# Tokens of both norms turned into columns by VectorE and DRAM scratch instead of TensorE

## The chip, the cores and the metric

The kernel runs on one core of a Trainium2 chip. The core has five engines that run side by side, each with a queue of its own that it works off in order: TensorE (PE in the profile: matmuls, and PEld for its weight loads), VectorE (DVE), ScalarE (ACT), GpSimd (POOL) and SyncE (SP, which here only issues transfers). Transfers between DRAM and the on-chip memory SBUF go through 16 DMA engines. TensorE writes its results to the on-chip memory PSUM, and VectorE and ScalarE read them there.

The metric is the time of one execution in device microseconds. Before the change three runs gave a median of 994.76 us (994.67 to 995.08).

## The reference

One decoder layer over 1024 tokens of width 1024, in float32:

```python
z = h @ w_in                                   # pool group | q | k | v
mix = concat([pool_mixer(z), sliding_window_attention(z)]) @ w_out
h = layer_norm(ALPHA * h + mix, ln1_g, ln1_b)            # norm 1
ff = square(relu(h @ w_ff1)) @ w_ff2
h = layer_norm(ALPHA * h + ff, ln2_g, ln2_b)             # norm 2
gate = sigmoid(h @ w_ple_gate + b_ple_gate)
out = h + gate * (p @ w_ple)
```

What matters here are the two norms. A norm runs along the 1024 channels of a token, so it wants tokens on the 128 partitions and channels along the row. The matmul that follows (with `w_ff1` after norm 1, with `w_ple_gate` after norm 2) sums over channels, so it wants channels on the partitions and tokens along the row: columns. Between norm and matmul each tile of 128 tokens has to be transposed.

## The kernel before

The tokens come in 8 tiles of 128 (`NT = 8`), the channels in 8 blocks of 128 (`NK = 8`). Products are accurate to more than one pass: each operand is split into a high part (`high`, a rounding copy on ScalarE, line 98) and the low rest (`low`, a subtraction on VectorE, line 103), and `mm3` (lines 113 to 115) makes three matmuls of them. The feed-forward part further saves products by a 2x2 scheme with seven products instead of eight (token halves by channel halves), which needs sums and differences of column blocks.

The work is written in Python with a tile framework. A planner orders the instructions of each engine's queue before the run, by the place in the program and by a simulated clock, and gives each tile a free buffer of its pool. So the written order is a priority; the order in the queues is fixed when the kernel runs. Where `tc.issue_after` stands, an instruction is queued behind a named one.

The buffers that matter: tag "n" (`nat`, 8 of 4 KB per partition), tag "ws" (`part` and `incoming`, 6), tag "c" (`big`, 6), tag "t" (`temp`, 6), and banks of PSUM ("mm", "pt", "av", "s" in the first half, "f" in the second).

**Around norm 1.** `out_left` and `out_right` multiply by `w_out` into the halves of the token tiles `hn[n]`, four tiles (one token half, t = 0 or 1) at a time. `norm1(n)` then runs `layer_norm(hn[n])` on VectorE with one step on ScalarE and one on GpSimd, and turns the tile into columns: `transposed` (line 427) makes four 128x128 transposes on TensorE into a PSUM bank, once for channel blocks 0 to 3 (`a`, bank "pt") and once for 4 to 7 (`b`, bank "av"). After that the tile is scaled by ALPHA and written to DRAM as the residual (`h_dram`). From `a` and `b` it makes splits: for t = 0 the operands "11" and "21", and a copy of `a` for three tiles in `pre`; for t = 1 the operand "22" and the differences "T1", "T2", "T3" (and later, in `last_sum`, "T4"). In the written order, tiles 0 to 3 come after `out_left(1)`; tiles 4 to 7 alternate with `early(p)`, which multiplies the first weights of `w_ff1` with "11" and then "21" and so needs tiles 0 to 3. The products that need the "T" operands follow after the last `early`; the first of them is `s2`, with "T2".

**Around norm 2.** The second feed-forward matmul runs as 56 units (seven products `i`, eight quarters `q`, `k` counting the quarters of a product), the last product being `i == 2`. Its results are added into `acc[n]` by `gather`. `norm2(n)` is written for tiles 0 to 3 during the last two products, and for tiles 4 to 7 after them. The gate's weights are loaded and split in `gate_load` during the last product. `gate_in(n)` makes the columns of tile n: eight transposes on TensorE into two PSUM banks "f", then split into the pair `h2`. In the last loop, per tile: `gate_in(n + 1)`, then `ple` (12 matmuls with `w_ple`) and `gate` (48 matmuls) and `result`, which ends in a store by SP.

SP issues nearly all loads, so it is one queue in which a load that waits for a free buffer holds those behind it.

Of the kernel before, what the change touches and what calls it, by code (L numbers as in the profile page):

```python
# [7 lines left out]
F32 = mybir.dt.float32  # L8
# [4 lines left out]
P = 128  # L13
# [54 lines left out]
def layer(ctx, tc, xT, x, pT, w_in, w_pool, pscale, sinks, w_out, ln1, w1, w2, ln2, w_ple, w_gate, bgate, bias, rcount, out):  # L68
# [7 lines left out]
    def nm(s):  # L76
        uid[0] += 1
        return f"{s}_{uid[0]}"
# [7 lines left out]
    def nat(shape, dt=F32):  # L86
        return sb.tile(shape, dt, tag="n", bufs=8, name=nm("n"))
# [8 lines left out]
    def high(dst, src, scale=None):  # L96
        if scale is None:
            nc.scalar.copy(out=dst, in_=src)  # L98
        else:
            nc.scalar.mul(out=dst, in_=src, mul=scale)  # L100

    def low(eng, dst, src, hi):
        return eng.tensor_tensor(out=dst, in0=src, in1=hi.bitcast(F32), op=ALU.subtract)  # L103
# [13 lines left out]
    def add(o, a, b, op=ALU.add):  # L117
        nc.vector.tensor_tensor(out=o, in0=a, in1=b, op=op)  # L118
# [13 lines left out]


    h_dram = [tc.dram_tile([P, D], F32, name=f"hd{n}") for n in range(NT)]
    f_dram = [tc.dram_tile([P, 2, 2, 2, HALF], F32, name=f"fd{q}") for q in range(NQUAD - NKEEP)]


# [30 lines left out]
    def tr_ps():  # L168
        return ps.tile([P, 4, P], F32, tag="pt", bufs=2, name=nm("pt"))
# [248 lines left out]
        nc.vector.scalar_tensor_tensor(out=y, in0=y, scalar=r, in1=gb[0], op0=ALU.mult, op1=ALU.mult)  # L418
        add(y, y, gb[1])

    def tr_av():
        return ps.tile([P, 4, P], F32, tag="av", bufs=1, name=nm("av"))

    def transposed(y, j, pt):
        for k in range(4):
            kt = 4 * j + k
            nc.tensor.transpose(pt[:, k, :], y[:, kt * P : (kt + 1) * P], ident)  # L427
        return pt
# [86 lines left out]

    X = {}

    def block(name, i, c):
        return X[name][:, i, :, c * P : (c + 1) * P].bitcast(F32)

    def split_to(name, c, src, eng):
        cs = slice(c * P, (c + 1) * P)
        dh = X[name][:, 0, :, cs]
        high(dh, src)
        return low(eng, X[name][:, 1, :, cs], src, dh)

    def norm1(n):
        t, c = n // 4, n % 4
        layer_norm(hn[n], gb1)
        a = transposed(hn[n], 0, tr_ps())  # L530
        b = transposed(hn[n], 1, tr_av())
        nc.scalar.mul(out=hn[n], in_=hn[n], mul=ALPHA)
        nc.scalar.dma_start(out=h_dram[n], in_=hn[n])
        if t == 0:
            if c < 3:
                nc.scalar.copy(out=pre[:, 4 + c].rearrange("p (k t) -> p k t", k=4), in_=a)
            split_to("11", c, a, nc.vector)
            split_to("21", c, b, nc.vector)
        else:
            r12, t1, t2 = temp((P, 4, P)), temp((P, 4, P)), nat([P, 4, P])  # L540
            nc.scalar.copy(out=r12, in_=a)
            if c < 3:
                add(t1, a, pre[:, 4 + c].rearrange("p (k t) -> p k t", k=4), ALU.subtract)
# [85 lines left out]
    def bank(shape=(P, HALF)):  # L629
        return pf.tile(list(shape), F32, tag="f", bufs=8, name=nm("f"))  # L630
# [178 lines left out]
    def gate_load(j):  # L809
# [5 lines left out]
        for k in range(2):  # L815
            load_split(w[:, 0, k], w[:, 1, k], src[k * P : (k + 1) * P, :], None, nc.vector, incoming((P, D)))

    def gate_in(n):
        h2 = [part((P, NK, P)) for _ in range(2)]
        for j in range(2):  # L820
            pt = transposed(acc[n], j, bank((P, 4, P)))
            dh = h2[0][:, 4 * j : 4 * j + 4, :]
            high(dh, pt)
            low(nc.vector, h2[1][:, 4 * j : 4 * j + 4, :], pt, dh)
        return h2

    def norm2(n):
# [9 lines left out]
    for u, (i, q) in enumerate(units):  # L837
        k = QORDER.index(q)
        if u < NQUAD - NKEEP:
            hidden[u] = big([P, 2, 2, 2, HALF], F32)  # L840
            nc.sync.dma_start(out=hidden[u], in_=f_dram[u])
        if u == 4:
            quarter = wide("pre", [P, 4, D], F32)
            for n in range(4):
                acc.append(quarter[:, n])
                nc.sync.dma_start(out=acc[n], in_=h_dram[n])
        if i == 5 and k == 2:
            residual_back(2)
        if 4 <= u + 3 < len(units):
            fetch(u + 3)  # L850
        if u + 1 < len(units):
            prepare(u + 1)
        if k == 0:
            banks_of[i] = banks_of[MERGE[i]] if i in MERGE else [bank() for _ in range(4)]
        if i == 2 and k == 7:
            h2s = [gate_in(0)]
        multiply(u, banks_of[i])
        if i != 2 or k >= 5:
            for _ in range(2 if i == 2 else 1):
                if pending:  # L860
                    with tc.issue_after(lows[-1].ins):
                        pending.pop(0)()
        if k == 7:
            pending += [lambda c=c, i=i: gather(i, c, banks_of[i][c]) for c in range(4)]
        if i == 6:
            if k == 0:
                gb2 = [incoming((P, D)) for _ in range(2)]
                for j in range(2):
                    nc.sync.dma_start(out=gb2[j], in_=ln2[j].partition_broadcast(P))
            if k in (3, 6):  # L870
                norm2(k // 3 - 1)
        if i == 2:
            if k in (1, 4):
                norm2(2 + k // 3)
            if k == 2:
                residual_back(2)
            if k >= 2:
                gate_load(k - 2)
    for piece in pending:
        piece()  # L880

# [4 lines left out]
    for n in range(NT):  # L886
        if n + 1 < NT:
            h2s.append(gate_in(n + 1))
        h2 = h2s[n]
        cols = [slice(0, HALF), slice(HALF, D)] if n < NT - 1 else [slice(0, HALF), slice(HALF, HALF + HALF // 2), slice(HALF + HALF // 2, D)]  # L890

        def ple(cs):
            o = bank()[:, 0 : cs.stop - cs.start]
            for k in range(2):
                pk = pTs[:, :, k, n * P : (n + 1) * P]
                mm3(o, pk[:, 0], pk[:, 1], wl[:, 0, k, cs], wl[:, 1, k, cs], k == 0, k == 1)
            return o

        def gate(cs):
            o = bank()[:, 0 : cs.stop - cs.start]  # L900
            for k in range(NK):
                w = gates[k // 2]
                mm3(o, h2[0][:, k, :], h2[1][:, k, :], w[:, 0, k % 2, cs], w[:, 1, k % 2, cs], k == 0, k == NK - 1)
            return o

        def result(cs, gt, pl):
            sg = temp()[:, 0 : cs.stop - cs.start]
            nc.vector.tensor_tensor(out=sg, in0=b3[:, cs], in1=gt, op=ALU.add)
            nc.scalar.activation(out=sg, in_=sg, func=AF.Sigmoid)
            nc.vector.tensor_tensor(out=sg, in0=sg, in1=pl, op=ALU.mult)  # L910
            nc.vector.tensor_tensor(out=sg, in0=sg, in1=acc[n][:, cs], op=ALU.add)
            nc.sync.dma_start(out=out[n * P : (n + 1) * P, cs], in_=sg)

        if n == 0:
            gts = [gate(cs) for cs in cols]
            for cs, gt in zip(cols, gts):
                result(cs, gt, ple(cs))
        else:
            for cs in cols:
                if cs.stop == D and n == NT - 1:  # L920
                    gt = gate(cs)
                    result(cs, gt, ple(cs))
                else:
                    pl = ple(cs)
                    result(cs, gate(cs), pl)
# [46 lines left out]
```

## Time and profile before

| what | value |
|---|---|
| median of three runs | 994.76 us (994.67 to 995.08) |
| span of the profiled execution, first to last instruction | 993.0 us |
| PE idle time that waits on other engines | four waits, the longest 1.4 us |
| PE, 860 to 910 us | busy 50.0 of 50 us |
| DVE, 860 to 910 us | busy 47.0 of 50 us |
| DVE, 300 to 320 us | busy 19.6 of 20 us |

The page gives the span of one profiled execution, the busy time of each engine, and the chain of work that ended last, followed back from the last instruction. Below it stand groups of instructions: line, engine, operation, what is written and read (names without numbers), count, then busy time in us, mean duration of one in ns, and the idle time of the engine just before. In a timeline the columns are start and duration in us, engine, line, operation, tiles, and how many neighbours were merged. Matmuls are pipelined: the next one starts before the last one's end, so the distance between starts tells more than a duration.

### The profile page before, as it was taken

How to read it: one execution, taken by the hardware profiler on the slowest of the kernel's cores; microseconds unless marked ns; L12 is line 12 of the kernel's file. 1: busy time of each engine (PE TensorE's matmuls, PEld its weight loads, DVE VectorE, ACT ScalarE, POOL GpSimd, SP SyncE). 2: the span in 40 equal slices, each digit the busy share in tenths (PEclk: the TensorE clock that was granted, in tenths of full speed). 3: DMA queues.
4: the chain of work that ended last, by engine and by line, in shares of the span. 5: the costliest groups of instructions: out<-in, count | busy, mean ns of one | idle time of the engine just before them, and what ended most of it. 6: DMA issues, size and time to landing. Idle time of an engine off the chain costs nothing.

```text
span 993.0 us, 12231 instructions
## 1 busy us (share of the span) xinstructions
PE 985.4 (99%) x4562; PEld 820.8 (83%) x4562; DVE 711.0 (72%) x1137; ACT 457.9 (46%) x737; POOL 105.6 (11%) x142
## 2 busy tenths in 40 slices
PE   9999999999999999999999999999999999999998
PEld 7888887888888888888888888888888888888887
DVE  5898888895869777564446756887647799896333
ACT  5676766543576443434444434433343454651111
POOL 0013562020000000100000000100111010000000
PEclk9999999999999999999999999999999999999999
DMA  6512142722161543742372993675798863721011
GB/s 218 181 64 85 45 147 85 233 82 89 66 238 57 191 149 149 198 163 106 118 274 96 343 330 101 181 227 201 207 212 186 217 157 118 215 73 43 35 40 43
DMA packets 39004, 148.01 MB, mean 149 GB/s; under 512 B 4768, under 2 KB 5920, under 8 KB 36128
## 3 DMA queue, kind: packets, MB, share of 16 engines
q1 hardware_dynamic: 29520, 115.90, 34.2%
q0 software_dynamic: 7840, 26.74, 11.4%
q10 hardware_dynamic: 1584, 4.59, 1.1%
q8 instruction: 36, 0.59, 0.2%
q14 instruction: 24, 0.20, 0.1%
HBM read 124.66 MB, written 22.54 MB: 148 GB/s over the span
## 4 chain that ended last, share of the span: by engine, by line
PE 98%; DVE 1%; POOL 1%; DMA 0%; issue 0%; ACT 0%; DVEq 0%
PE f L114 23%; PE f L115 23%; PE f L113 23%; PE mm L113 8%; PE mm L115 8%; PE mm L114 8%; PE pt L316 1%; PE s L293 1%; PE s L292 1%; PE f L427 1%; PE av L321 1%; PE av L322 1%; POOL h L360 0%; PE s L113 0%; PE s L114 0%; DMA n<-in_xT 0%
## 5 line engine op out<-in xcount | busy, mean ns | idle before, releaser
L113 PE MATMUL f<-c,ws 128*128 128x512 f32 (+1 forms) x456 | 175.8, 385 | 0.0
L114 PE MATMUL f<-c,ws 128*128 128x512 f32 (+1 forms) x456 | 175.7, 385 | 0.0
L115 PE MATMUL f<-c,ws 128*128 128x512 f32 (+1 forms) x456 | 175.2, 385 | 0.0
L115 PE MATMUL f<-x,w 128*128 128x512 f32 x448 | 174.3, 389 | 0.0
L114 PE MATMUL f<-x,w 128*128 128x512 f32 x448 | 174.3, 389 | 0.0
L113 PE MATMUL f<-x,w 128*128 128x512 f32 x448 | 147.1, 389 | 0.0
L98 ACT CAST w<-st 128x1024 fp32r<-128x1024 f32 (+2 forms) x66 | 65.7, 998 | 109.0 <-issue 69.9
L103 DVE TENSOR_TENSOR w<-st,w 128x1024 fp32r<-128x1024 f32 (+2 forms) x66 | 77.5, 1177 | 48.9 <-ACT w L98 48.8
L113 PEld LDWEIGHTS f<-c,ws 128*128 128x128 f32 x456 | 85.7, 188 | 17.2
L114 PEld LDWEIGHTS f<-c,ws 128*128 128x128 f32 x456 | 85.7, 188 | 17.1
L115 PEld LDWEIGHTS f<-c,ws 128*128 128x128 f32 x456 | 85.7, 188 | 17.1
L115 PEld LDWEIGHTS f<-x,w 128*128 128x128 f32 x448 | 84.1, 188 | 17.5
L114 PEld LDWEIGHTS f<-x,w 128*128 128x128 f32 x448 | 84.1, 188 | 17.5
L113 PEld LDWEIGHTS f<-x,w 128*128 128x128 f32 x448 | 84.0, 188 | 17.4
L98 ACT CAST ws<-w 128x512 fp32r<-128x512 f32 x60 | 37.1, 622 | 57.5 <-PE f L115 42.4
L103 DVE TENSOR_TENSOR x<-ws,x 128x1024 fp32r<-128x1024 f32 x52 | 63.4, 1218 | 0.0
L118 DVE TENSOR_TENSOR n<-t,f 128x512 f32<-128x512 f32 x48 | 31.9, 685 | 39.3 <-PE f L115 39.2
L103 DVE TENSOR_TENSOR ws<-w,ws 128x512 fp32r<-128x512 f32 x60 | 41.1, 689 | 25.1 <-ACT ws L98 24.7
L98 ACT CAST ws<-st 128x512 fp32r<-128x512 f32 x48 | 29.8, 621 | 60.1 <-PE f L115 35.2
L113 PE MATMUL mm<-c,w 128*128 128x512 f32 x144 | 56.4, 396 | 0.3 <-ACT w L98 0.3
L115 PE MATMUL mm<-c,w 128*128 128x512 f32 x144 | 56.5, 394 | 0.0
L114 PE MATMUL mm<-c,w 128*128 128x512 f32 x144 | 56.4, 393 | 0.0
(212 smaller groups left out, 1819.5 us busy)
## 6 DMA issues: line engine op xcount, KB each, us to landing
ws<-in_w SPq DMA_DIRECT2D x70, 512.0 KB, 3.9
w<-in_w SPq DMA_DIRECT2D x16, 1024.0 KB, 5.3
c<-fd SPq DMA_DIRECT2D x6, 2048.0 KB, 8.4
fd<-n POOLq DMA_DIRECT2D x20, 512.0 KB, 3.5
ws<-in_w POOLq DMA_DIRECT2D x20, 512.0 KB, 7.8
st<-in_w_in SPq DMA_DIRECT2D x17, 512.0 KB, 3.3
w<-in_w SPq DMA_DIRECT2D x10, 512.0 KB, 4.1
n<-in_x SPq DMA_DIRECT2D x8, 512.0 KB, 6.0
```

The source lines that it names most:

```text
L98: nc.scalar.copy(out=dst, in_=src)
L103: return eng.tensor_tensor(out=dst, in0=src, in1=hi.bitcast(F32), op=ALU.subtract)
L113: nc.tensor.matmul(o, ah, bh, start=first, stop=False, skip_group_check=more)
L114: nc.tensor.matmul(o, ah, bl, start=False, stop=False, skip_group_check=more)
L115: nc.tensor.matmul(o, al, bh, start=False, stop=last, skip_group_check=more)
L118: nc.vector.tensor_tensor(out=o, in0=a, in1=b, op=op)
L292: nc.tensor.matmul(s[:, i, dst], ql, kt[:, 0, g, kk : kk + kn], start=True, stop=False)
L293: nc.tensor.matmul(s[:, i, dst], ql, kt[:, 1, g, kk : kk + kn], start=False, stop=True)
L316: nc.tensor.transpose(pt[:, i, :], e[:, i, kb * P : (kb + 1) * P], ident)
L321: nc.tensor.matmul(av, VV[0][:, blk, g], pp[:, 0], start=(kb == lo), stop=False)
L322: nc.tensor.matmul(av, VV[0][:, blk, g], pp[:, 1], start=False, stop=(kb == 1))
L427: nc.tensor.transpose(pt[:, k, :], y[:, kt * P : (kt + 1) * P], ident)
```

## The change

`transposed` is left unused by both norms. A new function `flip` does its work without TensorE, in two steps. VectorE transposes each 32x32 block of the tile (its transpose works within 32 partitions and 32 columns) and puts the blocks in an order in which a later piece can be fetched in runs of 256 elements. SP then writes the tile to a scratch tensor in DRAM (`t_dram`, one per tile and norm) in one transfer, and reads it back in four, one for each group of 32 partitions, so that the blocks land in the partitions where they belong. The result lies in SBUF as (partition, R, k, c): token 32 R + c, channel 128 k + partition.

```diff
+    t_dram = [tc.dram_tile([P, 4, 2 * P], F32, name=f"td{n}") for n in range(2 * NT)]
...
-    def tr_av():
-        return ps.tile([P, 4, P], F32, tag="av", bufs=1, name=nm("av"))
+    def flip(y, b, t, d):
+        b4 = b.rearrange("p (q k c) -> p q k c", q=4, k=NK)
+        nc.vector.transpose(out=b4, in_=y.rearrange("p (k q r) -> p q k r", k=NK, q=4))
+        nc.sync.dma_start(out=d, in_=b.rearrange("p (q e) -> p q e", q=4))
+        for q in range(4):
+            nc.sync.dma_start(
+                out=t[32 * q : 32 * q + 32].rearrange("r (R e) -> r R e", R=4),
+                in_=d[:, q].rearrange("(R r) e -> r R e", R=4),
+            )
+        return t.rearrange("p (R k c) -> p R k c", R=4, k=NK)
```

Norm 1 calls it in the place of the transposes. For tiles 0 to 3 both buffers of `flip` are "ws" buffers; for tiles 4 to 7 the landing buffer is an "n" buffer. The splits and differences keep their number and read the columns from SBUF, in the new order of dimensions (`columns`, `quarters`):

```diff
     def norm1(n):
         t, c = n // 4, n % 4
         layer_norm(hn[n], gb1)
-        a = transposed(hn[n], 0, tr_ps())
-        b = transposed(hn[n], 1, tr_av())
+        ft = flip(hn[n], part((P, D), F32), nat([P, D]) if t else part((P, D), F32), t_dram[n])
+        a, b = ft[:, :, 0:4], ft[:, :, 4:8]
...
-                nc.scalar.copy(out=pre[:, 4 + c].rearrange("p (k t) -> p k t", k=4), in_=a)
+                nc.scalar.copy(out=quarters(pre[:, 4 + c]), in_=a)
```

Norm 2 gets a step of its own, `gate_flip`, with two "n" buffers, and `gate_in` becomes one split over all eight channel blocks instead of two over four:

```diff
+    flipped = {}
+
+    def gate_flip(n):
+        flipped[n] = flip(acc[n], nat([P, D]), nat([P, D]), t_dram[NT + n])
+
     def gate_in(n):
         h2 = [part((P, NK, P)) for _ in range(2)]
-        for j in range(2):
-            pt = transposed(acc[n], j, bank((P, 4, P)))
-            dh = h2[0][:, 4 * j : 4 * j + 4, :]
-            high(dh, pt)
-            low(nc.vector, h2[1][:, 4 * j : 4 * j + 4, :], pt, dh)
+        dh, dl = (h.rearrange("p k (R c) -> p R k c", R=4) for h in h2)
+        src = flipped.pop(n)
+        high(dh, src)
+        low(nc.vector, dl, src, dh)
         return h2
```

`gate_flip(0)` is written at `k == 4` of the last product, `gate_flip(1)` at its `k == 7` (just after `gate_in(0)`), and `gate_flip(n + 2)` in the last loop, just after `gate_in(n + 1)`.

More of the change, by code (lines that the diff above doesn't have):

```diff
@@ L516, in layer, with columns, quarters @@
     X = {}
+    def columns(name, i, c):
+        return X[name][:, i, :, c * P : (c + 1) * P].rearrange("p k (R c) -> p R k c", R=4)
     def block(name, i, c):
-        return X[name][:, i, :, c * P : (c + 1) * P].bitcast(F32)
+        return columns(name, i, c).bitcast(F32)
     def split_to(name, c, src, eng):
-        cs = slice(c * P, (c + 1) * P)
-        dh = X[name][:, 0, :, cs]
+        dh = columns(name, 0, c)
         high(dh, src)
-        return low(eng, X[name][:, 1, :, cs], src, dh)
+        return low(eng, columns(name, 1, c), src, dh)
+    def quarters(t):
+        return t.rearrange("p (R k c) -> p R k c", R=4, k=4)
     def norm1(n):
@@ L539, in norm1 @@
         else:
-            r12, t1, t2 = temp((P, 4, P)), temp((P, 4, P)), nat([P, 4, P])
+            r12, t1, t2 = quarters(temp()), quarters(temp()), quarters(nat([P, HALF]))
             nc.scalar.copy(out=r12, in_=a)
             if c < 3:
-                add(t1, a, pre[:, 4 + c].rearrange("p (k t) -> p k t", k=4), ALU.subtract)
+                add(t1, a, quarters(pre[:, 4 + c]), ALU.subtract)
             else:
@@ L856, in layer @@
             h2s = [gate_in(0)]
+            gate_flip(1)
         multiply(u, banks_of[i])
@@ L878, in layer @@
                 gate_load(k - 2)
+            if k == 4:
+                gate_flip(0)
     for piece in pending:
@@ L888, in layer @@
             h2s.append(gate_in(n + 1))
+        if n + 2 < NT:
+            gate_flip(n + 2)
         h2 = h2s[n]
```

## Prediction

> **What bounds the kernel now.** First the engine totals, the chain that ended last, and TensorE's own waits:
>
> ```profile
> span 993.0 us, 12231 instructions
> PE 985.4 (99%) x4562; PEld 820.8 (83%) x4562; DVE 711.0 (72%) x1137; ACT 457.9 (46%) x737; POOL 105.6 (11%) x142
> PE 98%; DVE 1%; POOL 1%; DMA 0%; issue 0%; ACT 0%; DVEq 0%
> PE pt L387 <- POOL ident masks.py:199: 1.4, 1, 1.4
> PE s L113 <- DVE sm L296: 1.2, 1, 1.2
> PE s L292 <- DVE sm L296: 0.9, 1, 0.9
> PE mm L113 <- ACT w L98: 0.3, 1, 0.3
> ```
>
> TensorE (PE) is busy for 99% of the span, carries 98% of the last chain, and in the whole run waits for other engines 1.4 + 1.2 + 0.9 + 0.3 = 3.8 us. A busy PE need not be full, but here the question is only whether it stands in line for anything, and it does not. So the time falls by what leaves PE's queue, as long as no new wait enters it.
>
> What leaves it are the 128 transposes of line 427. The groups by form give them, and PE's timeline gives what one really costs:
>
> ```profile
> L427 PE MATMUL av<-ident,n 128*128 128x128 f32 x32 | 4.8, 272 | 0.0
> L427 PE MATMUL pt<-ident,n 128*128 128x128 f32 x32 | 4.8, 272 | 0.0
> L427 PE MATMUL f<-ident,pre 128*128 128x128 f32 x32 | 4.1, 272 | 0.0
> L427 PE MATMUL f<-ident,n 128*128 128x128 f32 x32 | 4.1, 272 | 0.0
> ...
> 249.11 0.39 PE L113 MATMUL mm<-c,c 128*128 128x512 f32 x1
> 249.35 0.60 PE L427 MATMUL av<-ident,n 128*128 128x128 f32 x4
> 249.70 0.48 PE L114 MATMUL mm<-c,c 128*128 128x512 f32 x1
> 250.01 0.40 PE L115 MATMUL mm<-c,c 128*128 128x512 f32 x1
> ...
> 867.09 0.39 PE L115 MATMUL f<-x,w 128*128 128x512 f32 x1
> 867.32 1.03 PE L427 MATMUL f<-ident,pre 128*128 128x128 f32 x8
> 868.11 1.17 PE L113 MATMUL f<-x,w 128*128 128x512 f32 x4
> 869.12 0.40 PE L114 MATMUL f<-x,w 128*128 128x512 f32 x1
> ```
>
> Instructions overlap, so durations don't add: 512-column matmuls last 0.39 us but start 0.227 us apart (867.09 to 867.32). The price is the shift of later starts. **Norm 1**, four at a time: without the group the matmul of 249.70 would start at 249.35 and the next one 0.227 us on, at 249.58; it starts at 250.01. A group costs 0.43 us. **Norm 2**, eight at a time: four matmuls (4 x 0.227 = 0.91) from 867.32 would put the next at 868.23; it starts at 869.12. A group costs 0.89 us.
>
> **The change, term by term.**
>
> *Removed from PE.* Norm 1: 8 tiles x 2 groups x 0.43 = 6.9 us. Norm 2: 8 x 0.89 = 7.1 us. Together 14.0 us, 0.11 per transpose. [...]
>
> *Added on VectorE.* One 32x32-block transpose of 128x1024 per tile, 16 in all. No row shows one. The nearest are DVE passes over the same 1024 columns; the bounds are a pass over half of them below, and two whole passes above:
>
> ```profile
> L103 DVE TENSOR_TENSOR w<-st,w 128x1024 fp32r<-128x1024 f32 x60 | 74.5, 1244 | 48.9 <-ACT w L98 48.8
> L103 DVE TENSOR_TENSOR ws<-f,ws 128x512 fp32r<-128x512 f32 x16 | 10.7, 682 | 1.6 <-ACT ws L98 1.6
> ```
>
> Bounds 0.68 and 2.5 us; I take 1.2, so 16 x 1.2 = 19 us. Against it gate_in's two half-width subtractions become one (2 x 0.682 to 1.24), 0.12 us per tile; its two casts on ACT become one too. Norm 1's splits keep their number. The columns are read from SBUF instead of PSUM; the first row reads SBUF and the second PSUM, and half of 1244 is near 682, so I give that nothing.
>
> *Added transfers.* Per tile one write of 512 KB and four reads of 128 KB, five issues on SP, 80 in all. Nearest rows:
>
> ```profile
> hd<-n ACTq DMA_DIRECT2D x8, 512.0 KB, 2.6
> n<-hd SPq DMA_DIRECT2D x4, 512.0 KB, 5.8
> out<-t SPq DMA_DIRECT2D x15, 256.0 KB, 2.0
> L912 SPq DMA_DIRECT2D out<-t x17: 332/332/344, 891.0 to 990.4; - x17
> ```
>
> The last row: an issue holds SP 0.33 us. Write 2.6; the reads, 512 KB together, 2.0 (the 256 KB transfers to out) to 5.8 (n<-hd), and I take 3.5, near the middle, as the four move in parallel; issues 5 x 0.33 = 1.7. From the end of the norm to columns in SBUF: 1.2 + 2.6 + 3.5 + 1.7 = 9 us, with bounds 0.7 + 2.6 + 2.0 + 1.7 = 7 and 2.5 + 5.8 + 5.8 + 1.7 = 16. This latency takes the place of 0.4 to 0.9 us on PE, so each tile's slack decides.
>
> ```profile
> 226.00:233.00 7.00, 7.00 (x33) 5.79 (x32) 1.05 (x3) 0.00 (x0) 0.00 (x0) 1.00 0.26 80
> 225.11 1.22 DVE L118 TENSOR_TENSOR n<-n,st 128x1024 f32<-128x1024 f32 x1
> 269.35 1.22 DVE L118 TENSOR_TENSOR n<-n,st 128x1024 f32<-128x1024 f32 x1
> 259.63 0.39 PE L113 MATMUL mm<-c,ws 128*128 128x512 f32 x1
> 298.29 0.60 PE L427 MATMUL av<-ident,n 128*128 128x128 f32 x4
> 306.95 0.39 PE L113 MATMUL f<-c,ws 128*128 128x512 f32 x1
> 838.00:868.00 30.00, 30.00 (x138) 24.89 (x137) 25.55 (x25) 17.90 (x18) 0.00 (x0) 1.00 0.61 189
> 868.00:908.00 40.00, 40.00 (x192) 33.43 (x191) 39.78 (x75) 16.59 (x21) 3.11 (x4) 1.00 0.19 63
> 908.00:985.00 77.00, 77.00 (x370) 64.64 (x369) 27.50 (x42) 10.79 (x19) 0.00 (x0) 1.00 0.10 38
> ```
>
> In the stretches the columns are length, PE, weight load, DVE, ACT, POOL, granted clock (full, 1.00), DMA share, GB/s.
>
> *Norm 1, tiles 0 to 3: cover large.* The last of these norms ends at 226.3, and DVE then works only 1.05 us of the next seven, for the transposes wait behind out_left(1) in PE's order. The columns are first used by early(0), whose first matmul (259.63) starts near 256 after, 8 groups of 0.43 sooner. 226.3 + 9 = 235, or 242 at the worst bound; splits add 3. Nothing is late.
>
> *Norm 1, tiles 4 to 7: cover also large.* Tile 7's norm ends at 270.6, but its second group sits at 298.29, behind early products. VectorE needs no turn in PE's queue: columns at about 280, at worst 287. The first product that needs the differences made from them starts at 306.95, near 300 after. Their splits move forward out of a crowded stretch.
>
> *Norm 2.* Flips 0 and 1 meet a DVE with 4.5 us free before 868, and want 2.4. Then DVE is full (39.78 of 40 us) until 908, and flips 2 and 3 add 2.4 us to it, while PE comes sooner. The tightest use is tile 1:
>
> ```profile
> 884.26 1.27 DVE L103 TENSOR_TENSOR ws<-f,ws 128x512 fp32r<-128x512 f32 x2
> 874.46 0.48 PE L113 MATMUL f<-c,ws 128*128 128x512 f32 x1
> 890.41 0.39 PE L113 MATMUL f<-c,ws 128*128 128x512 f32 x1
> ```
>
> Its low half is ready at 885.5 and used at 890.4. Three groups (tiles 0, 1, 2) leave PE ahead of that use, so it comes 2.7 us sooner, 887.7, counting this stage alone. Up to three flips, 3.6 us of DVE, less 0.2, can stand before the subtraction: 885.5 to 888.9. Between nothing and 1.2 us late; PE has the second half's w_ple products (six matmuls, 1.4 us) to draw forward. I take 0.5 us. For tiles 4 to 7 PE takes about 14.8 us each (874.46 to 993 over eight tiles), more than a flip's 9, and DVE is idle 64% of that time (27.5 busy of 77): hidden. If that cover were gone, a late tile would show its whole excess on PE.
>
> *Buffers.* In norm 2 a flip takes two of eight "n" buffers; acc[4..7] and the gate's bias hold five, so three are left: the columns being split, and one flip in flight. That is one tile ahead, 14.8 us for a chain of 9 to 16; at the upper end the last tiles would be 1 us late each, about 6 in all, and I count that in the late-gate rival. In norm 1 the first four flips take two of six "ws" buffers each, which early(0) and early(1) want too, but not before 256.
>
> *SP.* SP runs in order: a write waits for the block transpose, the reads for the write's landing, and loads queued behind wait too. Other loads stand early, for what they wait on is mostly a free buffer:
>
> ```profile
> SPq L583 <- DVE ws L103: 53.6, 4, 44.6
> SPq L107 <- DVE c L103: 19.3, 10, 2.6
> ```
>
> L583 brings early's weights, L107 the gate's. I take no loss from them and keep it as a rival.
>
> **Sum.** 993.0 - 14.0 + 0.5 = 979.5 us of span. The median, 994.76, is 1.8 above the span, so **981.2 us**, between 980.7 with nothing late and about 983 with the bounds of these terms.
>
> **Rivals.** Each against 994.8.
>
> *Gate stage late.* DVE's full 40 us decides. If a block transpose costs 2.5 us, or a flip takes 16, or the planner puts the flips behind all four late norms, some tiles come 1 to 2 us late each, 2.5 to 6 us together: 983 to 987. For: 39.78 of 40. Against: low-priority work gets turns there (the subtraction at 884).
>
> *Handed back.* PE's operands might be only just in time while DVE is full (800 to 838, 868 to 908); then saved time returns as waits for splits. At worst all 14 us return: 987 to 994.8. That is also the case where the change moves PE's transposes without result. Against it:
>
> ```profile
> ACT w L98 <- PE f L115: 84.1, 30, 3.4
> ```
>
> The casts that feed PE wait for PE to free buffers, so they run ahead.
>
> *Slower: SP's order.* A flip holds SP for 2.6 + 1.7 = 4.3 us, with the wait for DVE 5.5. Six flips (tiles 4 to 7 of norm 1; 0 and 1 of norm 2) lie where SP feeds PE. Uncovered, 6 x 5.5 = 33 us: 1014. It decides from 14 us uncovered, 2.3 per flip. Against it, the waits for buffers above. [...]
>
> *More than the starts show.* Were PE held for each transpose's full 272 ns, 128 x 0.272 = 35 us would go: 960. The starts at 867.32 and 868.11, eight transposes in 0.79 us, speak against it. [...]
>
> **How the numbers follow.** Forecast (980.5 to 983) 0.66; gate stage late 0.15; handed back 0.08, of which half within 0.2% of before; slower by SP 0.05; below the forecast 0.06, with 0.01 of that for full durations. The range, 979.4 to 987, holds forecast and late gate, 0.81; its lower end lies 1.3 us under the full saving, a tenth of it, since two groups stand for 24. A measurement tells about 0.2% (2 us) from no change. Faster 0.91, same 0.04, slower 0.05.
>
> **What would show it.** PE: no line 427, matmul count down by 128, busy time and span down by about 14 us, waits still below 6 us in all. By 306.95's counterpart the first T2 product should start near 300, and tile 0's gate about 9 us earlier than 874.46. DVE: 16 transposes near 1.2 us. SP: five issues per tile, landings under 6 us. Wrong if PE shows waits named after column splits (ws, x, c) or weights behind SP, or if the block transposes take above 2 us. If the span falls by over 20 us, my price of a transpose was wrong.

## The result: 0.2% slower, and the profile after

The changed kernel takes 997.12 us (median of 17 runs, 994.76 to 998.48), the one before 994.73 (17 runs, 994.35 to 995.31): ratio 1.0023, 95% interval 1.0015 to 1.0030. The forecast was 981.2. The steps cost about what was forecast; the 14 us came back as waits of TensorE, and as slower matmuls behind two of them (0.43 us from start to start instead of 0.227). The profiled execution took 995.10 us, near the fastest of the 17. First the page of the changed kernel with its last chain, then its groups by form (norm 1's block transposes: busy us, mean ns), then TensorE's waits (total us, times, longest):

```profile
span 993.3 us, 12109 instructions
PE 977.0 (98%) x4434; PEld 808.7 (81%) x4434; DVE 726.1 (73%) x1145; ACT 459.3 (46%) x729; POOL 108.9 (11%) x142
PE 80%; DVE 7%; DMA 7%; issue 3%; ACT 1%; SPq 1%; POOL 1%; ACTq 0%; DVEq 0%; POOLq 0%
```

```profile
L424 DVE STREAM_TRANSPOSE ws<-n 128x1024 f32<-128x1024 f32 x8 | 9.9, 1238 | 0.0
```

```profile
PE mm L113 <- ACT pre L601: 2.3, 1, 2.3
PE f L114 <- DVE x L103: 2.2, 3, 1.0
PE f L113 <- ACT c L98: 1.9, 1, 1.9
...
PE mm L115 <- DVE ws L103: 1.1, 1, 1.1
PE mm L113 <- ACT ws L98: 1.1, 1, 1.1
```

128 matmul instructions are gone (4562 to 4434), and a block transpose costs 1.24 us, as assumed. But PE holds only 80% of the last chain (98% before). The waits shown here add 8.6 us, where before a single 0.3 us of such waits for operands stood. The stretches of the changed kernel say where (PE, PEld, DVE, ACT, POOL, granted clock, DMA share, GB/s):

```profile
260.00:280.00 20.00, 18.85 (x76) 15.19 (x75) 19.23 (x34) 16.19 (x29) 6.18 (x4) 0.91 0.70 237
...
300.00:320.00 20.00, 15.82 (x61) 12.27 (x60) 19.31 (x33) 11.80 (x21) 1.09 (x2) 0.91 0.23 90
...
838.00:880.00 42.00, 40.56 (x175) 32.25 (x174) 37.31 (x36) 22.05 (x23) 0.00 (x0) 1.00 0.63 203
```

PE is short of its full 20 and 42 us in all three, and its mean granted clock falls to 0.91 in the first two. Its timeline puts the idle at 258 to 262, 301 to 309 and 845 to 858 us, all ahead of the gate's stage, and 1.0 us more near 644 us, whose cause was not found.

**Near 260 us: early's weights come late.** The timeline of SyncE in the kernel before, with the issue of the raw weights of the first two products, then that of SyncE, ScalarE and TensorE in the changed kernel:

```profile
193.32 15.48 SPq L583 DMA_DIRECT2D ws<-in_w  x2
```

```profile
241.34 2.01 SPq L427 DMA_DIRECT2D ws<-td  x4
243.45 0.85 SPq L597 DMA_DIRECT2D ws<-in_w  x2
...
248.49 1.14 ACT L98 CAST c<-ws 128x512 fp32r<-128x512 f32 x2 [6.42 <-DMA ws<-td]
249.53 1.15 ACT L418 ACTIVATE n<-n,sm 128x1024 f32<-128x1024 f32 x1
250.59 1.12 ACT L98 CAST ws<-ws 128x512 fp32r<-128x512 f32 x2
...
259.64 0.50 PE L113 MATMUL mm<-c,ws 128*128 128x512 f32 x1 [1.14 <-ACT ws L98]
...
261.52 0.76 PE L115 MATMUL mm<-c,ws 128*128 128x512 f32 x1 [1.15 <-DVE ws L103]
262.08 0.63 PE L113 MATMUL mm<-c,ws 128*128 128x512 f32 x1
```

Before, the weights were fetched from 193 us on. Now they are issued at 243.45, directly behind tile 3's reads of scratch. ScalarE stands 6.42 us in line for the landing of those reads; tile 4's norm (L418) and the cast of the weights are queued behind. The products wait twice, and from 262.08 us on seven matmuls start 0.42 us apart instead of 0.227 and take up to 0.63 us instead of 0.39, at a granted clock of 0.50 (262 to 265 us).

**Near 303 us: tile 7's columns come late.** The timeline of VectorE, SyncE, ScalarE and TensorE in the changed kernel:

```profile
285.59 1.22 DVE L118 TENSOR_TENSOR n<-n,st 128x1024 f32<-128x1024 f32 x1
...
289.60 1.24 DVE L424 STREAM_TRANSPOSE ws<-n 128x1024 f32<-128x1024 f32 x1
...
290.87 0.33 SPq L425 DMA_DIRECT2D td<-ws  x1
...
294.34 1.85 SPq L427 DMA_DIRECT2D n<-td  x4
...
300.66 0.62 ACT L555 COPY t<-n 128x512 f32<-128x512 f32 x1 [3.25 <-DMA n<-td]
...
302.75 0.57 ACT L601 COPY pre<-mm 128x512 f32<-128x512 f32 x1
...
303.38 0.50 PE L113 MATMUL mm<-c,ws 128*128 128x512 f32 x1 [2.32 <-ACT pre L601]
...
308.29 0.73 PE L113 MATMUL f<-c,ws 128*128 128x512 f32 x2 [1.86 <-ACT c L98]
```

The norm ends at 286.8, not 270.6; its transpose starts 2.8 us later; write, reads and landing take to 300.66, 11.1 us from the transpose's start. ScalarE waits for it in order. Behind it in ScalarE's queue stands the copy at 302.75 of an early product's first result, which must be out of its PSUM bank before PE adds the second product to it. PE stops 2.32 us for that copy, though neither has anything to do with tile 7. The 1.86 us at 308.29 are of another kind: there the first T2 product waits for the high part of tile 7's own columns, whose differences and casts end 7 us behind the landing.

**Near 854 us** the same once more, smaller: the gate's weights go out at 849.64, before at 838.62. Three flips that the planner drew forward (tiles 0 to 2) precede them on SyncE, and ScalarE waits for the weights ahead of the units' casts (timeline of SyncE and ScalarE):

```profile
849.64 0.85 SPq L107 DMA_DIRECT2D ws<-in_w_gate  x2
...
853.86 1.05 ACT L98 CAST c<-ws 128x1024 fp32r<-128x1024 f32 x1 [7.04 <-DMA ws<-in_w_gate]
```

Of PE's two waits here, 0.78 us at 846.43 and 0.44 us at 858.49, only the second lies behind this cast; what made the first is not shown.

### The profile page after: what moved, and what is told of

It is laid out like the page before. It is cut to its first block, busy times and chain, and to the rows that moved or that the text cites. A ratio compares the mean times of both kernels' runs of the same rounds, so it can differ in the third digit from the quotient of the medians.

```text
span 993.3 us, 12109 instructions
## 1 busy us (share of the span) xinstructions
PE 977.0 (98%) x4434; PEld 808.7 (81%) x4434; DVE 726.1 (73%) x1145; ACT 459.3 (46%) x729; POOL 108.9 (11%) x142
## 4 chain that ended last, share of the span: by engine, by line
PE 80%; DVE 7%; DMA 7%; issue 3%; ACT 1%; SPq 1%; POOL 1%; ACTq 0%; DVEq 0%; POOLq 0%
PE f L114 20%; PE f L115 20%; PE f L113 20%; PE mm L113 5%; PE mm L114 5%; PE mm L115 5%; DMA td<-ws 2%; DVE w L103 1%; DVE x L103 1%; DMA n<-td 1%; PE pt L317 1%; DVE st L118 1%; DMA ws<-in_w 1%; DMA ws<-td 1%; DMA ws<-in_w_gate 1%
## 5 line engine op out<-in xcount | busy, mean ns | idle before, releaser
L113 PE MATMUL f<-c,ws 128*128 128x512 f32 (+1 forms) x456 | 176.3, 387 | 1.9 <-ACT c L98 1.9
L113 PE MATMUL f<-x,w 128*128 128x512 f32 x448 | 147.1, 389 | 0.1
L98 ACT CAST w<-st 128x1024 fp32r<-128x1024 f32 (+2 forms) x66 | 65.7, 998 | 105.0 <-issue 58.0
L113 PEld LDWEIGHTS f<-c,ws 128*128 128x128 f32 x456 | 85.9, 189 | 19.5 <-ACT c L98 2.3
L113 PEld LDWEIGHTS f<-x,w 128*128 128x128 f32 x448 | 84.0, 188 | 17.9 <-ACT x L98 0.6
L98 ACT CAST ws<-w 128x512 fp32r<-128x512 f32 x60 | 37.2, 620 | 56.4 <-PE f L115 47.4
L113 PE MATMUL mm<-c,w 128*128 128x512 f32 x144 | 56.3, 395 | 0.1
L98 ACT CAST x<-ws 128x1024 fp32r<-128x1024 f32 x52 | 54.5, 1047 | 0.0
```

The source lines that it names most:

```text
L113: nc.tensor.matmul(o, ah, bh, start=first, stop=False, skip_group_check=more)
```

## The experiments

Theory: the transfers cost what the transposes gave back, since engines that work their queues in order wait for landings, and the weight loads stand behind the transfers on SyncE and behind the "ws" buffers that they hold. Rival 1: VectorE's 16 x 1.24 us push norms and splits. Rival 2: one resource alone does it (SyncE's order, or the buffers, or the bytes). Edits are against the changed kernel. Each time stands beside runs of the kernel before on the same chip (994.7 to 994.9 us).

### Which norm, and transfers or VectorE

**norm1_only** and **norm2_only**: the other norm gets back its `transposed` code from before.

> Norm 1's columns by VectorE pieces and DRAM scratch, norm 2's by TensorE as before. In the changed kernel's trace the first product after norm 1 starts 1.3 us later than before and the first unit 3.1 us later, though 6.9 us of transposes are gone. If each norm's stage pays for itself: 994.7 + 3 = 997 to 998.5 us, with TensorE idle again near 258 to 261 and 300 to 309 us and its clock down behind both. Rival (the two stages share a cost, such as VectorE's total load): clearly under 996.

Measured 1003.59 us, ratio 1.0081 (1.0060 to 1.0102).

> Norm 2's columns by VectorE pieces and DRAM scratch, norm 1's by TensorE as before. The changed kernel's gate stage has no idle of its own; its units lose some 2.5 to 4 us between 845 and 880 us. If the stages are separate: 994.7 - 7.1 + 2.5 to 4 = 990 to 991.5 us. Rival (norm 2's transfers cost all that its transposes cost): 994 or more.

Measured 989.81, ratio 0.9951 (0.9936 to 0.9966). So norm 2 pays, 4.9 us of its 7.1, and norm 1 loses 8.9 instead of gaining 6.9. I had expected a loss of 3 there; its waits show PE standing 5.5 us at once:

```profile
PE mm L113 <- ACT pre L601: 5.5, 1, 5.5
```

The two effects add to +4.0, the whole change has +2.4. The 1.6 us between lie within norm1_only's interval (6.0 to 10.1 us slower), so these runs show no effect of one stage on the other.

**no_trip**

```diff
-        nc.sync.dma_start(out=d, in_=b.rearrange("p (q e) -> p q e", q=4))
-        for q in range(4):
-            nc.sync.dma_start(
...
-        return t.rearrange("p (R k c) -> p R k c", R=4, k=NK)
+        return b.rearrange("p (R k c) -> p R k c", R=4, k=NK)
```

> All 16 block transposes by VectorE stay, the transfers are left out: the columns are read straight from the transposed pieces, so that the output is that of wrongly placed columns. If the transfers cost the time (they stand in the order of SyncE's queue, and ScalarE waits in order for their landings): 981 to 985 us. If VectorE's added 16 x 1.24 us cost it (norms and casts late): 993 or more.

Measured 981.18, ratio 0.9865 (0.9848 to 0.9881). From its page, and of its waits the only one that the kernel before lacks:

```profile
span 979.4 us, 11956 instructions
PE 971.1 (99%) x4434; PEld 807.4 (82%) x4434; DVE 726.6 (74%) x1145; ACT 459.1 (47%) x729; POOL 106.9 (11%) x142
```

```profile
PE f L114 <- DVE x L103: 0.7, 1, 0.7
```

This is the forecast to the tenth, with VectorE as loaded as in the changed kernel (726.6 and 726.1 us). Rival 1 falls: VectorE's load alone costs nothing. What the transfers cost, with the waits they bring and the landing buffers (which this kernel doesn't take either), is 997.1 - 981.2 = 15.9 us. In the profiled executions PE does the same 4434 matmuls; the changed kernel has it idle 8.0 us longer (16.3 against 8.3) and busy 5.9 us longer (977.0 against 971.1), where matmuls behind the waits run slower (up to 0.63 us each instead of 0.39, from 262 and from 309 us on).

### SyncE's order, buffers, bytes

**gp_queue**: in `flip`, `nc.sync.dma_start` becomes `nc.gpsimd.dma_start`, five times per tile.

> The changed kernel with its 16 writes and 64 reads issued by GpSimd in place of SyncE. If what costs the time is that weight loads stand behind the transfers in SyncE's order: 985 to 990 us, the gate's weights again loaded from 838 us on. If it is the landings themselves, for which ScalarE and VectorE wait in order, and the buffers that the pieces hold: 994 to 998 us, with the same idle of TensorE near 303 and 308 us.

Measured 995.05, ratio 1.0001 (0.9992 to 1.0011): 2 us better than the change, no more. PE's long wait stays, and is longer; it is now the one for tile 7's own columns:

```profile
PE f L113 <- ACT c L98: 5.7, 1, 5.7
```

But this kernel doesn't take the order of a queue away, it puts another in its place. GpSimd also stores the early products' results (line 607), and the timeline of GpSimd has two such stores, which wait for ScalarE, between tile 7's write and its reads:

```profile
288.00 0.55 POOL L425 DMA_DIRECT2D td<-ws  x1
296.78 0.54 POOL L607 DMA_DIRECT2D fd<-t  x1 [8.23 <-ACT t L592]
...
300.19 2.24 POOL L427 DMA_DIRECT2D n<-td  x4 [0.19 <-issue]
```

The reads go out 12.2 us behind the write, where SyncE in the changed kernel took 3.5 (290.87 to 294.34). So these 2 us don't tell what SyncE's order costs while columns are waited for. And the gate's weights still go out late, at 848.03, with SyncE waiting 6.4 us for a buffer: SyncE's order isn't the only reason there.

**idle_trip**: all transfers run, but nobody waits for their landing.

```diff
-        return t.rearrange("p (R k c) -> p R k c", R=4, k=NK)
+        return b.rearrange("p (R k c) -> p R k c", R=4, k=NK)
```

> The changed kernel with all its block transposes, writes and reads, but the columns are taken from the transposed pieces themselves, so that no instruction waits for a landing (the output is that of wrongly placed columns). If the cost lies in the wait for landings: 981 to 984 us, as without the transfers (981.2). If it lies in SyncE's order, the buffers that the transfers hold and the bytes on the DMA engines: 990 to 997 us.

Measured 991.59, ratio 0.9968 (0.9954 to 0.9983). The second expectation holds, near its lower end: some 5.5 us go with the consumers' waits, and 10.4 us stay that the transfers cost by merely running, with the order of SyncE, the bytes and the buffers that they bring. (The split is rough, as the pieces are held until the splits here.) Three kernels take one thing each away from idle_trip. **idle_gp** issues the transfers by `nc.gpsimd.dma_start`. **idle_room** and **idle_thin** (its reads are cut to `[:, :, 0:32]` likewise):

```diff
-        ft = flip(hn[n], part((P, D), F32), nat([P, D]) if t else part((P, D), F32), t_dram[n])
+        ft = flip(hn[n], part((P, D), F32), nat([P, D]) if t else pre[:, 0:2].rearrange("p j e -> p (j e)"), t_dram[n])
```

```diff
-        nc.sync.dma_start(out=d, in_=b.rearrange("p (q e) -> p q e", q=4))
+        nc.sync.dma_start(out=d[:, :, 0:32], in_=b.rearrange("p (q e) -> p q e", q=4)[:, :, 0:32])
```

> The changed kernel with all transfers, no landing waited for by a consumer (columns taken from the transposed pieces), and the transfers issued by GpSimd. idle_trip had 991.6 with them on SyncE, the kernel without transfers 981.2. If SyncE's order makes the 10 us between: 981 to 985 us. If the buffers or the bytes make them: 990 to 993 us.

> As idle_trip (transfers on SyncE, no landing waited for by a consumer), but the targets of norm 1's tiles 0 to 3 lie in two empty slices of pre, so that these tiles take one buffer of ws each, as in the kernel without transfers. If the second buffer of ws makes the idle near 258 to 262 us: that idle (3.5 us and the slow clock behind it) goes, 986 to 988.5 us. If SyncE or the bytes make it: 990 to 993 us.

> As idle_trip, but each row of each write and read carries an eighth of its elements (the same instructions, waits and buffers; scratch is written in part). If the bytes on the DMA engines (0.91 busy from 280 to 300 us) hold back the weights: 983 to 987 us. If SyncE's order and the buffers do: 989.5 to 993 us.

Measured 984.86 (ratio 0.9898, 0.9882 to 0.9915), 984.56 (0.9896, 0.9882 to 0.9911) and 984.27 (0.9897, 0.9882 to 0.9912). I had expected one of the three to cure it; each alone did, by 7 us. The issue of early's raw weights in the timeline of SyncE shows what they have in common; idle_trip first, then idle_gp, idle_room and idle_thin:

```profile
246.32 0.85 SPq L597 DMA_DIRECT2D ws<-in_w  x2
```

```profile
234.47 16.20 SPq L597 DMA_DIRECT2D ws<-in_w  x2
```

```profile
231.56 0.35 SPq L597 DMA_DIRECT2D ws<-in_w  x1
243.71 0.42 SPq L597 DMA_DIRECT2D ws<-in_w  x1
```

```profile
238.33 0.85 SPq L597 DMA_DIRECT2D ws<-in_w  x2
```

Each brings the first product's weights forward, by 8 to 15 us (those of the second go out at 250.34 in idle_gp, later than in idle_trip). That fits one chain with the three as its links: a transfer's turn on SyncE, its bytes, the release of its "ws" buffer, the load of the weights. The chain is argued from these rows and not shown link by link: front4, below, has its weights as late as 244.81 and no idle near 261. Rival 2 falls as well for this part of the loss: no one of the three makes the loss by itself, for without any one of them most of it is gone. The 3 to 4 us that remain above no_trip are several small waits, different in each kernel; they were not followed further.

### Which tiles of norm 1

**front4** (tiles 0 to 3) and **back4** (tiles 4 to 7); norm 2 by TensorE in both. The edit of front4; back4 has `t == 1`:

```diff
-        ft = flip(hn[n], part((P, D), F32), nat([P, D]) if t else part((P, D), F32), t_dram[n])
-        a, b = ft[:, :, 0:4], ft[:, :, 4:8]
+        if t == 0:
+            ft = flip(hn[n], part((P, D), F32), nat([P, D]) if t else part((P, D), F32), t_dram[n])
+            a, b = ft[:, :, 0:4], ft[:, :, 4:8]
+        else:
+            a, b = (transposed(hn[n], j, r()).rearrange("p k (R c) -> p R k c", R=4) for j, r in enumerate((tr_ps, tr_av)))
```

> Only norm 1's tiles 0 to 3 take the new way; tiles 4 to 7 and all of norm 2 are transposed by TensorE as before. Eight groups of transposes (8 x 0.43 = 3.5 us) go. If these tiles' pieces and columns in the buffers named ws delay the first product's weights: TensorE idles 1.3 us or more near 261 us and gives most of it back, 993 to 995.5 us, without the idle near 300. If the loss sits in tiles 4 to 7 alone: 991 to 992 us.

Measured 993.35, ratio 0.9986 (0.9976 to 0.9995). Of 3.5 us 1.5 remain. The weights are late here too (SyncE, 244.81 us), yet in the profiled execution (992.43 us, the fastest of ten) there is no idle near 261; one new wait stands near 235, 0.6 us (`PE mm L113 <- DVE n L452`), where VectorE's residual addition is late.

> Only norm 1's tiles 4 to 7 take the new way. 3.5 us of transposes go. If the landing of tile 7's columns, for which ScalarE and VectorE wait in order, is what costs: TensorE idles 4 to 8 us between 290 and 313 us, its clock falls behind it, 996 to 1002 us. If the trouble there only followed from the delay of tiles 0 to 3: 991 to 992 us.

Measured 996.89, ratio 1.0017 (1.0007 to 1.0027): 3.5 us of transposes gone, and 2.0 slower. The timeline of ScalarE and TensorE:

```profile
299.16 0.62 ACT L98 CAST x<-n 128x512 fp32r<-128x512 f32 x1 [3.72 <-DMA n<-td]
...
302.76 0.58 ACT L607 COPY pre<-mm 128x512 f32<-128x512 f32 x1
...
303.40 0.50 PE L113 MATMUL mm<-c,ws 128*128 128x512 f32 x1 [2.76 <-ACT pre L607]
...
304.36 0.63 PE L113 MATMUL mm<-c,ws 128*128 128x512 f32 x1
```

The landing at 299.16, the copy behind it and PE behind the copy: the second wait needs no help from tiles 0 to 3. Loss against the full saving: 2.0 us for front4, 5.5 for back4, 15.8 for all eight (13 to 17 by norm1_only's interval). Together the halves cost about twice their sum. A likely reason, not tested apart, is that what delays the first tiles delays the norms of the others: tile 4's norm ends at 248.8 in back4 and at 256.1 in the changed kernel, tile 7's at 282.5 and 286.8.

**front4_room**: pieces and columns of tiles 0 to 3 both in empty slices of `pre`.

```diff
-            ft = flip(hn[n], part((P, D), F32), nat([P, D]) if t else part((P, D), F32), t_dram[n])
+            ft = flip(hn[n], *(pre[:, 2 * j : 2 * j + 2].rearrange("p j e -> p (j e)") for j in range(2)), t_dram[n])
```

> As front4, but the pieces and the columns of tiles 0 to 3 lie in the four slices of the tile pre that stand empty until the first products end (their only use before), so that no buffer of ws is taken. If the buffers held up the weights: the raw weights are loaded near 193 to 208 us as before, no idle near 261, 990.5 to 992 us. If SyncE's order or VectorE held them up: as front4.

Measured 994.99, ratio 1.0004 (0.9993 to 1.0014): a miss for both. The weights are fetched at 194 us as before, and yet the kernel is no faster than front4. With one slice for all pieces, each transpose has to wait for the last tile's write (at 235.36 VectorE stands 1.20 us for it), and VectorE's residual additions, in order behind it, come too late for PE's next bank (timeline of VectorE and TensorE):

```profile
235.36 1.25 DVE L427 STREAM_TRANSPOSE pre<-n 128x1024 f32<-128x1024 f32 x1 [1.20 <-DMA td<-pre]
236.53 1.25 DVE L452 SCALAR_TENSOR_TENSOR n<-n,mm 128x512 f32<-128x512 f32 x2
...
237.23 0.50 PE L113 MATMUL mm<-c,c 128*128 128x512 f32 x1 [2.51 <-DVE n L452]
```

### Norm 2's tiles, and versions that keep what pays

**gate6**: norm 1 by TensorE, of norm 2 tiles 2 to 7 the new way; `gate_in` takes the old path for a tile that isn't in `flipped`.

```diff
-            gate_flip(1)
...
-            if k == 4:
-                gate_flip(0)
```

> Norm 2's tiles 2 to 7 take the new way, with every transfer inside the gate's stage; its tiles 0 and 1 and all of norm 1 are transposed by TensorE. 6 x 0.89 = 5.3 us go. If norm 2's loss came from the two early flips that stand ahead of the gate's weights and the units' casts: 989 to 990 us and the idle of 845 to 860 us gone. If the gate's stage itself costs something: 990.5 us or more.

Measured 989.51, ratio 0.9945 (0.9930 to 0.9959): 5.4 us, all that six tiles can give (5.3). The gate's stage shows no cost, and the idle of 845 to 860 us is gone. The flips of tiles 0 and 1, and what they draw forward, save 1.8 us of transposes in norm2_only and cost about 2.3 (the two kernels lie 0.5 us apart, within their intervals).

**front4_gate6** joins the two.

> Norm 1's tiles 0 to 3 and norm 2's tiles 2 to 7 take the new way, the other six tiles TensorE. If the stages add up: 993.4 + 989.5 - 994.9 = 988.0 us. Rival (the two compete for a resource after all): 989.5 or more, no better than norm 2's six tiles alone.

Measured 987.87, ratio 0.9927 (0.9912 to 0.9941), 0.1 from the sum.

**front4_skew_gate6** and **skew_gate6**: `norm1` is cut behind the store of the residual, and its second half, `use1`, is written one tile later. Both have the first edit; in skew_gate6 all of norm 1 goes by `flip`, and the second edit sets tiles 4 to 7.

```diff
     for n in range(4):
         norm1(n)
+        if n:
+            use1(n - 1)
+    use1(3)
```

```diff
-        if p % 2 and p // 2 < 4:
+        if p in (1, 2, 4, 6):
             norm1(4 + p // 2)
+        if p in (2, 4, 6, 7):
+            use1({2: 4, 4: 5, 6: 6, 7: 7}[p])
```

> As front4_gate6, but the columns of each of norm 1's tiles 0 to 3 are used one tile later in the program, behind the next tile's norm. If ScalarE's and VectorE's waits for the landings push the later norms and casts: 985.5 to 987 us, 0.5 to 1.5 us less than without. If the chain of buffers named ws or SyncE decides there: as front4_gate6, 988 us, or later, since each buffer is held longer.

Measured 988.27, ratio 0.9931 (0.9917 to 0.9946): no gain over front4_gate6.

> All of norm 1 and norm 2's tiles 2 to 7 take the new way; the columns of norm 1's tiles are used one tile later, and the norms of tiles 5 to 7 come one or two products sooner. If waiting for landings in order makes the loss (8.9 us where norm 1 alone was changed): 983 to 987 us and no idle near 300 us. If buffers, SyncE or VectorE's load make it: 995 us or more.

Measured 994.79, ratio 0.9999 (0.9990 to 1.0008). By the parts, norm1_only and gate6, 998.2 was due without the skew, so it won about 3.4, not the 11 or more of its first expectation, by which waiting in order is the whole loss. (Each buffer is also held longer here, so this doesn't part the two causes.) In its waits the long ones come back (at 277 and 309 us of its timeline):

```profile
PE mm L113 <- ACT pre L608: 3.0, 2, 2.8
PE f L114 <- DVE c L103: 2.8, 1, 2.8
```

**front4_gate7**: front4_gate6 with `gate_flip(1)` written behind the last unit, ahead of `norm2(4)`.

> front4_gate6 and, of norm 2, tile 1 by the new way too, its transfers issued behind the last unit. 0.9 us of transposes more go. If tile 1's columns land before its products (13.6 us after the first tile's start): 986.8 to 987.3 us. If they come late or hold the gate's loads: 987.9 us or more.

Measured 986.76, ratio 0.9921 (0.9906 to 0.9935): 1.1 us less than front4_gate6, where 0.9 were due, though the intervals overlap.

**front4_half_gate7**: the same, with only the landed columns of tiles 0 to 3 in `pre`, in two slices by turns; **front7_half_gate7**: that, with `n < 7` for `t == 0`.

```diff
-            ft = flip(hn[n], part((P, D), F32), nat([P, D]) if t else part((P, D), F32), t_dram[n])
+            ft = flip(hn[n], part((P, D), F32), nat([P, D]) if t else pre[:, n % 2 * 2 : n % 2 * 2 + 2].rearrange("p j e -> p (j e)"), t_dram[n])
```

> As front4_gate7 (986.8 us), but the landed columns of norm 1's tiles 0 to 3 lie in empty slices of pre, two by turns, so that each tile takes one buffer of ws in place of two. If what the first tiles still lose (2.8 us gained of 3.5) hangs on that buffer: 985.5 to 986.3 us. If it hangs on the residual additions that VectorE does late near 234 us: 986.5 to 987.5 us.

Measured 986.74, ratio 0.9918 (0.9905 to 0.9932): no change. The residual's wait near 235, 1.5 us in front4_gate7's profiled execution, is gone from this one. The 0.8 us of `PE mm L113 <- ACT c L98` on its page stand at 8.6 us, in the kernel's first products, and have nothing to do with the norms. So the time is the second expectation's, but its reason, the late residual additions, doesn't show in this execution.

> As front4_half_gate7, and norm 1's tiles 4, 5 and 6 by the new way too; only tile 7, whose landing the next stage waits for, stays with TensorE. 6 x 0.43 = 2.6 us of transposes more go. If tile 7's chain alone made the idle near 300 us: 983 to 985 us. If any landing between 260 and 300 us, or VectorE's load there, gives it back: 987 us or more.

Measured 987.28, ratio 0.9928 (0.9914 to 0.9941). Three tiles more take 2.6 us off PE and give it all back, so it isn't tile 7's chain alone; waits that front4_half_gate7 doesn't have stand at 264, 280, 301 and 306 us (TensorE's, of this kernel; the first row has three of them):

```profile
PE mm L113 <- ACT pre L607: 2.8, 3, 1.3
PE f L114 <- DVE c L103: 1.4, 1, 1.4
```

Of the kernels whose columns land where they belong, eight beat both the kernel before and the changed one. The fastest are front4_gate7 and front4_half_gate7, 986.7 us, 8 us under the time before, though the intervals of front7_half_gate7, front4_gate6 and front4_skew_gate6 overlap with theirs. These two use VectorE and scratch for eleven of sixteen tiles, TensorE for norm 1's tiles 4 to 7 and norm 2's tile 0.

## Why the prediction was wrong

*The saving: right.* 14.0 us were due, and no_trip, without the transfers, gains 13.5: 981.18 us against a forecast of 981.2. The price by distance between starts (0.43 and 0.89 us a group) held, that by duration (35 us) did not. That the tenths agree is luck: the forecast held 0.5 us for a late gate, and no_trip has 0.7 us of stall near 633 us instead.

*VectorE: right.* 1.24 us against 1.2, and its load did no harm.

*The transfers' sizes: right.* The write and the reads land in 2.9 to 3.2 us (medians of the traces; taken 2.6 and 3.5), and tile 7's chain takes 11.1 us, within the 7 to 16.

*"Norm 1, tiles 4 to 7: cover also large": the step that failed.* It set 9 us behind the norm's end of before, 270.6, and came to about 280, with 300 as the time of use. It took for granted that the norm would end as before and that the transpose would get its turn at once. The columns landed at 300.66, 21 us later: 16.2 of them because the norm ended only at 286.8, 2.8 because the transpose waited for its turn on VectorE, and 2.1 because the chain took 11.1 us and not 9. The norm's delay comes with the transfers. Without them it ends at 271.9, as before, and even a transpose 11.5 us behind it hurts nobody (no_trip's timeline of VectorE):

```profile
270.71 1.22 DVE L118 TENSOR_TENSOR n<-n,st 128x1024 f32<-128x1024 f32 x1
...
283.38 1.24 DVE L424 STREAM_TRANSPOSE ws<-n 128x1024 f32<-128x1024 f32 x1
```

How a landing delays a norm is seen for tile 4 above: ScalarE's step of the norm (L418) stands behind casts that wait for tile 3's columns. back4 shows the price of tiles 4 to 7: 5.5 us lost, where 3.5 were to be saved.

*"Norm 1, tiles 0 to 3: cover large", and the buffers that early wants "not before 256": failed.* 256 is when the product starts. Its raw weights wanted the buffers from 193 us on. idle_room, with one buffer of "ws" less per tile, won 7 us on idle_trip; where the columns are waited for, front4_half_gate7 won nothing by the same.

*"SP. I take no loss": failed, and the rival that should have caught it was too narrow.* It priced SyncE being held, 33 us for six flips, and gave it 0.05. The loss was 16 us, just past its point of 14, and its price was not how long SyncE is held: idle_gp, idle_room and idle_thin each win 7 us by freeing SyncE, a buffer or the DMA engines, as long as nobody waits for the landings. How much SyncE's order costs where they are waited for stays open, since gp_queue's reads stand behind GpSimd's stores. The loads that wait early for buffers (53.6 us) were read as slack of SyncE; what they wait for is just what the change hands to the flips.

*What was not in the sum at all:* that the waiting engine holds others. The plan asked for each column whether it lands before its own product. In the changed kernel only 1.86 us of PE's waits are of that kind (308.29); 2.32 us were for the copy `pre<-mm` and 2.3 us for the weights' high and low parts near 260, which were loaded late and stood behind a waiting ScalarE, and two stretches at a granted clock of 0.50 cost some 1.6 us each (below).

*The rival "handed back"* named the outcome, saved time that returns as waits, but put it where VectorE is full (800 to 838, 868 to 908). PE was held elsewhere, by landings.

*The gate's stage: pessimistic.* 0.5 us was taken; gate6 shows none. Norm 2's loss (2.2 us) goes with the flips of tiles 0 and 1, before it, in the units.

*What would show it* named waits for "ws, x, c" and weights behind SP and a limit of 6 us of waits: those signs appeared. Still open are a stall of 0.4 to 1.0 us near 640 us, which many kernels with a changed norm 1 have (no_trip too, 0.7), and what made the 0.78 us at 846.43.

## What to carry to other kernels

A transfer that replaces work of the bounding engine has to land early for the first instruction behind the one that waits, on every engine that waits in order, and not only for its own consumer: here the landing at 300.66 us held ScalarE's copy until 302.75, and TensorE stopped 2.32 us for that copy. For each buffer that a detour takes, look up when the next owner's load was issued before, not when its product ran. Where a change works in one stage and not in another, keep it where every landing has an idle queue behind it: here that was worth 8 us, where the whole change cost 2.4.

## What the runs showed of the hardware

A wait was paid twice where the clock followed. Behind the idle at 303 and 308 us the changed kernel's matmuls start 0.43 us apart instead of 0.227 for 3.4 us. The granted clock is 0.50 from 309.50 to 312.80 us, and 1.00 from 303 to 309 and from 313 to 320. The first and last rows of that stretch in TensorE's timeline:

```profile
309.33 0.58 PE L113 MATMUL f<-c,ws 128*128 128x512 f32 x1
309.70 0.63 PE L114 MATMUL f<-c,ws 128*128 128x512 f32 x1
...
312.69 0.44 PE L115 MATMUL f<-c,ws 128*128 128x512 f32 x1
```

Seven such distances (309.70 to 312.69, 0.427 each) cost 7 x 0.2 = 1.4 us, with the edges about 1.6. Such a stretch came in six of the twenty kernels traced, the first 8 us left out (there starts lie up to 0.59 us apart in the kernel before and 0.49 in the changed one, at a granted clock of 1.00). It came behind 2.8 us of idle (back4, and skew_gate6 at 277) to 5.7 us (gp_queue), and behind shorter ones close together: 1.14 + 1.15 us with two matmuls between (above, 262.08), and 2.32 + 1.86 us, 5 us apart (here). It did not come behind 2.51 us in front4_room or 2.8 us at 309 in skew_gate6, where the granted clock is 1.00 (233 to 260 and 300 to 320 us), nor behind any single idle of 1.6 us (the longest of these, in gp_queue and idle_gp) or less. In norm1_only, with idle of 5.5 and 1.9 us, the mean granted clock from 300 to 320 us is 0.74, against 0.91 in the changed kernel.

Landings vary much within one execution: the changed kernel's writes of scratch in norm 1 and their reads took 2.4 us at least, 3.1 in the middle and 8.9 at most. Those of 7.2 us and more were issued from 221 to 222 us; why they took so long was not followed. And kernels with such waits scatter: 3.7 us from lowest to highest in the changed kernel's 17 runs, 1.0 in those of the kernel before.
